# A two-block transformer on one Trainium2 core: where runs of filler matmuls, weight splits and index scores stand in the attention layers

## The chip, the core and the metric

The program runs on one core of one Trainium2 chip. A core has five engines that work side by side, each through its own instruction queue in order: TensorE (PE: matrix products and transposes), VectorE (DVE), ScalarE (ACT), GpSimd (POOL) and SyncE (SP, which here only starts DMA transfers). They wait for one another by semaphores. The metric is the time of one execution on the device in microseconds (us).

## The reference

The input is one sequence of 256 tokens of width 1024, with a memory of 256 rows, all in fp32. Two blocks follow one another. The first has two layers, and each is half a feed-forward part, a mixer and half a feed-forward part; the second has an attention mixer and an expert part. Cut to what matters here:

```python
for i in range(2):                                   # first block
    mem_k, mem_v = split(mem_n @ mem_w_kv[i])
    x = x + 0.5 * swiglu(rmsnorm(x, g0), w_up, w_down)
    h = rmsnorm(x, g1)
    mix = pool_layer(...) if i == 0 else diff_layer(...)
    x = x + mix
    x = x + 0.5 * swiglu(rmsnorm(x, g2), w_up, w_down)

def diff_layer(h, ...):                              # 8 heads, two softmaxes each
    o = (softmax(q1 k1) - lam * softmax(q2 k2)) @ v
    o = rmsnorm(o, norm_g) * (1 - lam_init)
    xo = memory_attention(xq, mem_k, mem_v)          # 4 heads over the memory
    return concat([o, xo]) @ w_out

def hybrid_mixer(h, ...):                            # second block
    # 8 heads over all earlier tokens, 8 heads over the tokens of an index
    score = sum_h iw[h] * relu(iq[h] @ ik)           # 4 index heads
    keep  = top_k(where(causal, score, -inf), 64)    # per query row
    y = concat([moba_attention(...), dsa_attention(..., keep)])
    return y @ w_out
```

## The kernel before, in words

All activations stay on the chip. A matrix product in fp32 is done as three matmuls (`mm3`, L207 to L209) on a high and a low part of both factors. The weights come in chunks of 128 x 1024 values by DMA (`load_to`, L127) as `raw`; ScalarE rounds each to `whi` (`split_one`, L157), VectorE subtracts to get `wlo` (`low_one`, L137; `low_all` does all that are due). The program is one order written out by the Python code: each engine works through its instructions in the order in which the code issues them, so moving a call moves its instructions on every engine that it uses.

In the attention layers a cursor `fill` walks through products that have time (the projections of the next group of heads, then the output product `out_proj_k`), in runs; one `step(fill)` issues one run, and most runs split one chunk ahead (`ahead_one`: `low_all`, then one `split_one`). `pipeline(units, ...)` (L44) walks through the attention units (a unit is a token tile of 128 rows `t` and a pair or group of heads), each cut in steps: s0 scores, bias, row maximum and exponentials; s1 the division by the row sums; s2 the transposes of the probabilities and the copy `pt`; s3 the product with the values; in the diff layer s4 to s6 norm the heads' outputs and transpose them into `cat`. In each tick it takes one step of several units, with two gaps in a tick, and the list `counts` (L993 in the diff layer, L1244 in the second block) says how many runs of `fill` go in each gap.

`out_proj_k` (L420) ends the layers. It adds its product to the rows `x`, half a row (512 columns) at a time, and prepares the following norm: `nxt.pre` scales the half row, `nxt.T` transposes it into `hT_hi` and `hT_lo`, which are what the next block multiplies. A plain norm (`nxt.deep` is false) follows the pool layer and the diff layer.

In the second block `select(t)` computes the index scores of token tile `t` (scores, then eight pairs of MAX and MATCH_REPLACE on VectorE in four steps, then the mask M). Its steps are taken among the runs of the first `aq` and `ak` projections (L1235) and then in the first ticks of the units.

Of the kernel before, what the change touches and what calls it, by code (L numbers as in the profile page):

```python
# [45 lines left out]
def pipeline(units, order):  # L46


    for tick in range(len(units) + max(d for _, d in order)):
        for s, d in order:  # L50
            if s is None:
                yield
                continue
            n = tick - d
            if 0 <= n < len(units) and s < len(units[n]):
                units[n][s]()
        yield
# [3 lines left out]
def kernel(ctx: ExitStack, tc: tile.TileContext, A, LAY, stop=None):  # L61
# [11 lines left out]
    def pmm():  # L73
        return ps.tile([P, 512], F32, name="mm", tag="mm", bufs=4)

    def ptr():
        return ps.tile([P, 512], F32, name="tr", tag="tr", bufs=2)
# [53 lines left out]
    def low_one():  # L131

        j, r, p_ = st["low"].pop(0)
        c = st["s"][j]
        nk, w = items[j][1:3]
        lo = p_.tile([P, CH], F32R, name="wlo", tag="wlo", bufs=4)
        V.tensor_tensor(lo[:, :nk * w], r[:, :nk * w], c.hi.rearrange("p k w -> p (k w)").bitcast(F32), op=OP.subtract)  # L137
        c.lo = lo[:, :nk * w].rearrange("p (k w) -> p k w", w=w)

    def low_all():  # L140
        while st["low"]:
            low_one()

    def split_one():

        j = st["split"]
        load_to(j + cfg["raw"] - len(st["low"]))
        _, nk, w, call = items[j][:4]
        n = nk * w
        r = st["raw"].pop(j)  # L150
        if call is not None:
            call(r[:, :n].rearrange("p (k w) -> p k w", w=w))
        else:
            p_ = wpool2 if j < dense and st["nsplit"] % 2 else wpool
            st["nsplit"] += 1
            hi = p_.tile([P, CH], F32R, name="whi", tag="whi", bufs=4)
            ACT.activation(hi[:, :n], r[:, :n], AF.Copy)  # L157
            st["s"][j] = Split(hi[:, :n].rearrange("p (k w) -> p k w", w=w), None)
            st["low"].append((j, r, p_))
        st["split"] += 1  # L160
        while st["low"] and not cfg["spread"]:
            low_one()
        load_to(j + 1 + cfg["raw"] - len(st["low"]))
# [16 lines left out]
    def ahead_one():  # L180

        if cfg["spread"] and st["split"] < min(st["use"] + 5, len(items)):
            low_all()
            split_one()

    def split_more(n):
        for _ in range(n):
            split_one()

    def fetch(n):  # L190
        got, k = [], 0
        for _ in range(n):
            c, nk, w = nextw()
            got += [(c, kk, k + kk) for kk in range(nk)]
            k += nk
        return got
# [3 lines left out]
    def run_deferred():  # L200
        while deferred:
            deferred.pop(0)()
        for f in strip_hook:
            f()

    def mm3(out, a, b, start, stop):
        PE.matmul(out, a[0], b[0], start=start, stop=False)  # L207
        PE.matmul(out, a[0], b[1], start=False, stop=False)  # L208
        PE.matmul(out, a[1], b[0], start=False, stop=stop)  # L209
# [37 lines left out]
    def proj_cols(act, n, n_ct, evac):  # L247
        got = fetch(n)
        for c0 in range(0, n_ct, 2):
            p = pmm()  # L250
            m = min(2, n_ct - c0)
            for j in range(m):
                if j:
                    ahead_one()
                    yield
                low_all()
                proj_col(act, got, c0 + j, p[:, j * S:(j + 1) * S])
            evac(c0, m, p[:, :m * S].rearrange("p (j t) -> p j t", t=S))
            ahead_one()
            yield  # L260
        run_deferred()
# [6 lines left out]
    def tr(out, in_):  # L268
        PE.transpose(out, in_, ident)
# [150 lines left out]
    def out_proj_k(segs, update, nxt, tail=2, ahead=None):  # L420


        p = [[pmm() for _ in range(2)] for _ in range(NT)]
        n = len(segs)

        def mm(t, h, gis, gots):
            for gi in gis:
                act, k0 = segs[gi]
                for c, k, _ in gots[gi][h]:
                    mm3(p[t][h], act[:, k0 + k, t * P:(t + 1) * P], c[:, k, :], gi == 0 and k == 0, gi == n - 1 and k == 1)  # L430

        gots = {}
        for gi in range(n - tail):
            gots[gi] = [fetch(1), fetch(1)]
            for t in range(NT):
                low_all()
                for h in range(2):
                    mm(t, h, [gi], gots)
                if t:
                    run_deferred()  # L440
                ahead_one()
                yield
        was = dict(cfg)
        cfg.update(ahead=8 - 2 * tail)
        for gi in range(n - tail, n):
            gots[gi] = [fetch(1), fetch(1)]
        cfg.update(was)
        while cfg["spread"] and nxt.deep and st["split"] < st["use"] + 4:
            split_one()
            low_all()  # L450
        for t in range(NT):
            for h in range(2):
                cut = n - 1 if nxt.deep and t and h else n
                mm(t, h, range(n - tail, cut), gots)
                if cut < n:
                    was = dict(cfg)
                    cfg.update(ahead=0)
                    ahead.append(fetch(4))
                    nxt.realT(0)
                    mm(t, h, range(cut, n), gots)  # L460
                    if tail > 2:
                        split_more(1)
                update(t, h, p[t][h])
                nxt.pre(t, h)
                if not nxt.deep and (t or h):
                    nxt.T(*((0, 0), (0, 1), (1, 0))[2 * t + h - 1])
                if h:
                    nxt.stats(t)
                if cut < n:
                    ahead.append(fetch(4))  # L470
                    cfg.update(was)
                if not nxt.deep:
                    ahead_one()
                yield
        if not nxt.deep:
            nxt.late = [lambda: nxt.T(1, 1)]
# [48 lines left out]
    def ffn(n, nxt, stk):  # L525
# [45 lines left out]
        if nxt.deep:  # L571
            flush()
            drain(out_proj_k([(gT, 2 * i) for i in range(11)], half_add, nxt, 3, nxt.got))
        else:
            out_proj(gT, 22, [4, 4, 3], half_add, nxt, first=flush)
# [53 lines left out]
    def step(*gens):  # L629
        for g in gens:  # L630
            next(g, None)
# [155 lines left out]
    with pool("pl") as sp:  # L787
# [53 lines left out]
        counts = [0, 1, 1, 0, 1, 1, 1, 2] + [1] * 6  # L841
# [21 lines left out]
    with pool("df") as sp:  # L863
# [120 lines left out]
        def qk(dst):  # L984
# [5 lines left out]
        o = out_proj_k([(cat, i) for i in range(0, 12, 2)], plain_add, n5)  # L990
        fill = itertools.chain(qk(k[1]), qk(q[1]), v_part(1),
                               proj_cols(hT, 4, 4, lambda c0, m, p: ACT.activation(qx[:, c0:c0 + m, :], p, AF.Copy)), o)
        counts = [1] * 9 + [2, 0, 1, 0, 0, 2, 1, 1, 1, 0, 0] + [1, 0] * 2 + [1, 1, 0, 1, 0, 2]  # L993
        for i, _ in enumerate(pipeline(units, [(5, 6), (1, 2), (4, 4), (None, 0), (6, 6), (0, 0), (3, 3), (2, 2)])):
            for _ in range(counts[i] if i < len(counts) else 1):
                step(fill)
# [147 lines left out]
    def col_evac(dst, b):  # L1144
        return lambda c0, m, p: ACT.activation(dst[:, 4 * b + c0:4 * b + c0 + m, :], p, AF.Copy)
# [81 lines left out]
    se = [select(0), select(1)]  # L1227
    for i, _ in enumerate(itertools.chain(proj_cols(hT, 4, 4, col_evac(aq, 0)), proj_cols(hT, 4, 4, col_evac(ak, 0)))):
        if i == 0:
            for t in range(NT):  # L1230
                q_ = ptr()
                tr(q_[:, :P], iks[t].rearrange("p a b -> p (a b)"))
                ACT.activation(ikT[:, t * P:(t + 1) * P], q_[:, :P], AF.Copy)
        else:
            step(*(se if i == 1 else se[1:] if i == 7 else se[:1]))  # L1235
    nhh = iter(("aq", "ak"))
    m2 = ModNorm(1, None, lambda t: sp.tile([P, D], F32, name="hh2", tag=next(nhh), bufs=1))
    o = out_proj_k([(yA, 0), (yA, 2), (yB, 0), (yB, 2)], Gated(g1), m2, 2, m2.got)
    fill = itertools.chain(proj_cols(hT, 4, 4, col_evac(aq, 1)), proj_cols(hT, 4, 4, col_evac(ak, 1)), v_part(), o)
    units = [make(t, g) for h in range(2) for t in range(NT) for g in (2 * h, 2 * h + 1)]  # L1240
    counts = [1, 0] + [1] * 7 + [0, 2, 0, 1, 0, 2, 0, 1, 0, 2, 1, 0, 0]
    for i, (n, _) in enumerate(zip(counts, pipeline(units, [(1, 2), (None, 0), (3, 3), (2, 2), (0, 0)]))):
        for _ in range(n):
            step(fill)  # L1244
# [306 lines left out]
    for i, (kind, arg) in enumerate(quanta):  # L1551
# [11 lines left out]
        n, t = arg[:2]  # L1563
# [105 lines left out]
def build(nc, arrays, lay, stop=None):  # L1669
    aps = {n: nc.dram_tensor(f"in_{n}_dram", a.shape, mybir.dt.from_np(a.dtype), kind="ExternalInput").ap()  # L1670
           for n, a in arrays.items()}
    aps["out"] = nc.dram_tensor("out_0_dram", (1, S, D), F32, kind="ExternalOutput").ap()
    with tile.TileContext(nc) as tc:
        kernel(tc, aps, lay, stop)
# [11 lines left out]
```

## Time and profile before

| | |
|---|---|
| Time, median of 3 runs | 2088.95 us (2086.64 to 2096.9) |
| The profiled execution | 2091.45 us, of which the span of the trace is 2089.3 us |
| TensorE busy | 2029.2 us, 97% of the span |
| VectorE busy | 1451.0 us, 69% |
| ScalarE busy | 991.4 us, 47% |
| TensorE's granted clock, mean | 0.993 of full speed |

The share of busy time is an average. What a stage costs is read from the gaps of the engine that is busy most, here TensorE: in a timeline of one engine each row has its start, its duration, and in brackets how long the engine was idle before it and what it waited for. The stages that the change touches are the end of the pool layer (about 325 to 360 us of the span), the diff layer's units and end (730 to 912 us) and the second block's attention (1120 to 1245 us).

### The profile page before, as it was taken

How to read it: one execution, taken by the hardware profiler on the slowest of the kernel's cores; microseconds unless marked ns; L12 is line 12 of the kernel's file. 1: busy time of each engine (PE TensorE's matmuls, PEld its weight loads, DVE VectorE, ACT ScalarE, POOL GpSimd, SP SyncE). 2: the span in 40 equal slices, each digit the busy share in tenths (PEclk: the TensorE clock that was granted, in tenths of full speed). 3: DMA queues.
4: the chain of work that ended last, by engine and by line, in shares of the span. 5: the costliest groups of instructions: out<-in, count | busy, mean ns of one | idle time of the engine just before them, and what ended most of it. 6: DMA issues, size and time to landing. Idle time of an engine off the chain costs nothing. (4 is left out here: it accounts for less than half of the span.)

```text
span 2089.3 us, 34420 instructions
## 1 busy us (share of the span) xinstructions
PE 2029.2 (97%) x13678; PEld 1824.7 (87%) x13678; DVE 1451.0 (69%) x2280; ACT 991.4 (47%) x1524; POOL 42.4 (2%) x74
## 2 busy tenths in 40 slices
PE   8999999999999998999999989999999999999998
PEld 7999888998899797789978768999998888888886
DVE  6677566776587557765646888889975666666666
ACT  6444454444344445444444554455554444444444
POOL 2000000000000000000001000000000000000000
PEclk9999999999999999999999999999999999999999
DMA  7667545666577653365544343656776776776764
GB/s 275 213 242 254 189 138 191 240 236 237 190 247 242 212 164 101 117 221 186 204 135 164 112 152 101 192 181 223 244 249 206 220 227 206 230 248 217 223 214 138
DMA packets 142377, 416.92 MB, mean 200 GB/s; under 512 B 12468, under 2 KB 47428, under 8 KB 140040
## 3 DMA queue, kind: packets, MB, share of 16 engines
q1 hardware_dynamic: 102672, 372.04, 53.2%
q10 hardware_dynamic: 37976, 36.91, 5.5%
q0 software_dynamic: 1568, 5.77, 0.9%
q8 instruction: 107, 1.75, 0.3%
q14 instruction: 54, 0.44, 0.1%
HBM read 396.82 MB, written 17.86 MB: 198 GB/s over the span
## 5 line engine op out<-in xcount | busy, mean ns | idle before, releaser
L137 DVE TENSOR_TENSOR wlo<-raw,whi 128x1024 fp32r<-128x1024 f32 (+1 forms) x654 | 784.1, 1221 | 331.3 <-ACT whi L157 330.5
L157 ACT ACTIVATE whi<-raw 128x1024 fp32r<-128x1024 f32 (+1 forms) x654 | 666.1, 1048 | 131.1 <-PE mm L209 66.5
L209 PE MATMUL mm<-hT_hi,wlo 128*128 128x256 f32 x1680 | 472.7, 281 | 8.6 <-DVE wlo L137 8.6
L207 PE MATMUL mm<-hT_hi,whi 128*128 128x256 f32 x1680 | 478.3, 285 | 0.0
L208 PE MATMUL mm<-hT_lo,whi 128*128 128x256 f32 x1680 | 471.7, 281 | 0.0
L209 PEld LDWEIGHTS mm<-hT_hi,wlo 128*128 128x128 f32 x1680 | 317.2, 189 | 10.1 <-DVE wlo L137 10.1
L207 PEld LDWEIGHTS mm<-hT_hi,whi 128*128 128x128 f32 x1680 | 317.3, 189 | 6.1 <-issue 5.5
L208 PEld LDWEIGHTS mm<-hT_lo,whi 128*128 128x128 f32 x1680 | 317.4, 189 | 2.0 <-issue 1.9
L207 PE MATMUL sm<-hT_hi,whi 128*128 128x256 f32 (+1 forms) x1048 | 299.7, 286 | 5.0 <-DVE hT_hi L215 2.5
L209 PE MATMUL sm<-hT_hi,wlo 128*128 128x256 f32 (+1 forms) x1048 | 297.1, 283 | 4.3 <-DVE wlo L137 4.3
L208 PE MATMUL sm<-hT_lo,whi 128*128 128x256 f32 (+1 forms) x1048 | 296.9, 283 | 0.4 <-DVE hT_lo L218 0.4
L207 PEld LDWEIGHTS sm<-hT_hi,whi 128*128 128x128 f32 (+1 forms) x1048 | 199.5, 190 | 8.3 <-DVE hT_hi L215 2.9
L207 PE MATMUL mm<-whi,wh 128*128 128x512 f32 x512 | 202.6, 396 | 2.0 <-ACT wh L217 2.0
L209 PEld LDWEIGHTS sm<-hT_hi,wlo 128*128 128x128 f32 (+1 forms) x1048 | 199.9, 191 | 4.7 <-DVE wlo L137 4.7
L209 PE MATMUL mm<-whi,wl 128*128 128x512 f32 x512 | 202.2, 395 | 0.0
L208 PE MATMUL mm<-wlo,wh 128*128 128x512 f32 x512 | 202.2, 395 | 0.0
L208 PEld LDWEIGHTS sm<-hT_lo,whi 128*128 128x128 f32 (+1 forms) x1048 | 199.3, 190 | 2.9 <-DVE hT_lo L218 0.6
L217 ACT ACTIVATE wh<-wf 128x256 fp32r<-128x256 f32 x128 | 53.5, 418 | 214.9 <-DVE wf L1535 214.9
L207 PE MATMUL mm<-whi,gT_hi 128*128 128x512 f32 x352 | 139.9, 397 | 0.0
L209 PE MATMUL mm<-whi,gT_lo 128*128 128x512 f32 x352 | 139.1, 395 | 0.0
L208 PE MATMUL mm<-wlo,gT_hi 128*128 128x512 f32 x352 | 139.0, 395 | 0.0
L1367 ACT ACTIVATE act<-sm 128x256 f32<-128x256 f32 x128 | 49.2, 385 | 167.9 <-PE sm L209 167.9
(308 smaller groups left out, 2605.4 us busy)
## 6 DMA issues: line engine op xcount, KB each, us to landing
raw<-in_ffn_up_dram SPq DMA_DIRECT2D x176, 512.0 KB, 5.2
raw<-in_peer_u_dram SPq DMA_DIRECT2D x128, 512.0 KB, 4.1
raw<-in_peer_v_dram SPq DMA_DIRECT2D x128, 512.0 KB, 3.7
raw<-in_ffn_dn_dram SPq DMA_DIRECT2D x88, 512.0 KB, 5.1
raw<-in_w_ada_dram SPq DMA_DIRECT2D x48, 512.0 KB, 4.8
gall<-stage ACTq DMA_DIRECT2D x16, 1024.0 KB, 4.8
G<-gall ACTq DMA_DIRECT2D x16, 1024.0 KB, 7.4
raw<-in_diff_w_in_dram SPq DMA_DIRECT2D x28, 512.0 KB, 4.3
```

The lines of the kernel that those rows point to most:

```text
L137: V.tensor_tensor(lo[:, :nk * w], r[:, :nk * w], c.hi.rearrange("p k w -> p (k w)").bitcast(F32), op=OP.subtract)
L157: ACT.activation(hi[:, :n], r[:, :n], AF.Copy)
L207: PE.matmul(out, a[0], b[0], start=start, stop=False)
L208: PE.matmul(out, a[0], b[1], start=False, stop=False)
L209: PE.matmul(out, a[1], b[0], start=False, stop=stop)
L217: ACT.activation(hi, src, AF.Copy)
L1367: ACT.activation(act[n], p, AF.Gelu)
```

## The change

Three edits of order; no operation is added or left out, and the queues of SP and POOL hold the same instructions in the same order as before.

- `out_proj_k`: what is due of `wlo` is done before each product of the tail. With a plain norm, the split of a next chunk (`ahead_one`) stands right behind the product instead of after the norm's work, and for the last half row `wlo` of that chunk follows at once. Between the norm's sums and the last `hT_lo` VectorE's queue then holds four `wlo` at the end of the diff layer, where it held six, and three at the end of the pool layer, where it held five; the others stand ahead of the updates of `x`.
- `counts` of the diff layer: from the tenth gap on, where a gap had two runs and others had none, these are spread, one run a gap.
- The second block: the index scores of tile 1 start one run later (with run 2 instead of run 1, so that tile 0 goes first), and the last of tile 1's pairs move into the ticks of the units; `counts` there has one run in places that had two, and one in places that had none.

```diff
--- before.py
+++ after.py
@@ -451,7 +451,12 @@
         for t in range(NT):
             for h in range(2):
                 cut = n - 1 if nxt.deep and t and h else n
+                low_all()
                 mm(t, h, range(n - tail, cut), gots)
+                if not nxt.deep:
+                    ahead_one()
+                    if t and h:
+                        low_all()
                 if cut < n:
                     was = dict(cfg)
                     cfg.update(ahead=0)
@@ -469,8 +474,6 @@
                 if cut < n:
                     ahead.append(fetch(4))
                     cfg.update(was)
-                if not nxt.deep:
-                    ahead_one()
                 yield
         if not nxt.deep:
             nxt.late = [lambda: nxt.T(1, 1)]
@@ -990,7 +993,7 @@
         o = out_proj_k([(cat, i) for i in range(0, 12, 2)], plain_add, n5)
         fill = itertools.chain(qk(k[1]), qk(q[1]), v_part(1),
                                proj_cols(hT, 4, 4, lambda c0, m, p: ACT.activation(qx[:, c0:c0 + m, :], p, AF.Copy)), o)
-        counts = [1] * 9 + [2, 0, 1, 0, 0, 2, 1, 1, 1, 0, 0] + [1, 0] * 2 + [1, 1, 0, 1, 0, 2]
+        counts = [1] * 9 + [1, 1, 1, 0, 1, 0, 1, 1, 1, 1, 0] + [1, 0] * 2 + [1, 1, 0, 1, 0, 2]
         for i, _ in enumerate(pipeline(units, [(5, 6), (1, 2), (4, 4), (None, 0), (6, 6), (0, 0), (3, 3), (2, 2)])):
             for _ in range(counts[i] if i < len(counts) else 1):
                 step(fill)
@@ -1232,13 +1235,13 @@
                 tr(q_[:, :P], iks[t].rearrange("p a b -> p (a b)"))
                 ACT.activation(ikT[:, t * P:(t + 1) * P], q_[:, :P], AF.Copy)
         else:
-            step(*(se if i == 1 else se[1:] if i == 7 else se[:1]))
+            step(se[i == 2])
     nhh = iter(("aq", "ak"))
     m2 = ModNorm(1, None, lambda t: sp.tile([P, D], F32, name="hh2", tag=next(nhh), bufs=1))
     o = out_proj_k([(yA, 0), (yA, 2), (yB, 0), (yB, 2)], Gated(g1), m2, 2, m2.got)
     fill = itertools.chain(proj_cols(hT, 4, 4, col_evac(aq, 1)), proj_cols(hT, 4, 4, col_evac(ak, 1)), v_part(), o)
     units = [make(t, g) for h in range(2) for t in range(NT) for g in (2 * h, 2 * h + 1)]
-    counts = [1, 0] + [1] * 7 + [0, 2, 0, 1, 0, 2, 0, 1, 0, 2, 1, 0, 0]
+    counts = [1, 0] + [1] * 7 + [0, 1, 1, 1, 0, 1, 1, 1, 0, 1, 1, 1, 0]
     for i, (n, _) in enumerate(zip(counts, pipeline(units, [(1, 2), (None, 0), (3, 3), (2, 2), (0, 0)]))):
         for _ in range(n):
             step(fill)
```

Three places of VectorE's queue (DVE) show what moves. A row reads line, operation, output<-inputs, shape and how many in a row; after the change lines behind L476 stand three higher, so L925 is L928 there. `pt` is the copy of the transposed probabilities (s2), `rc` and `e<-e,rc` are step s1, `ms` and `ov` belong to the norm of the heads (s4, s5), `cat_hi` to s6, and `e<-nd,sm` is the next unit's score.

The first place is in VectorE's queue of the diff layer, in the tick where token tile 0 begins its last two units; before:

```order
L925 COPY pt<-tr 128x512
L137 TENSOR_TENSOR wlo<-raw,whi 128x1024 x2
L907 RECIPROCAL rc<-sum 128x2
L908 RECIPROCAL rc<-sum 128x2
L909 TENSOR_SCALAR rc<-rc,nlam 128x2
L911 TENSOR_SCALAR e<-e,rc 128x256 x2
L913 SCALAR_TENSOR_TENSOR e<-e,rc 128x256 x2
L275 TENSOR_SCALAR ms<-oss 128x4
L891 SCALAR_TENSOR_TENSOR e<-nd,sm 128x128 x4
```

The same place of VectorE's queue now:

```order
L928 COPY pt<-tr 128x512
L137 TENSOR_TENSOR wlo<-raw,whi 128x1024
L910 RECIPROCAL rc<-sum 128x2
L911 RECIPROCAL rc<-sum 128x2
L912 TENSOR_SCALAR rc<-rc,nlam 128x2
L914 TENSOR_SCALAR e<-e,rc 128x256 x2
L916 SCALAR_TENSOR_TENSOR e<-e,rc 128x256 x2
L275 TENSOR_SCALAR ms<-oss 128x4
L137 TENSOR_TENSOR wlo<-raw,whi 128x1024
L894 SCALAR_TENSOR_TENSOR e<-nd,sm 128x128 x4
```

The second `wlo` has moved from ahead of step s1 to behind it.

The second place is some twenty rows further on in the same queue; before:

```order
L925 COPY pt<-tr 128x256
L952 TENSOR_TENSOR ov<-ov,ro 128x512
L907 RECIPROCAL rc<-sum 128x2
L908 RECIPROCAL rc<-sum 128x2
L909 TENSOR_SCALAR rc<-rc,nlam 128x2
L911 TENSOR_SCALAR e<-e,rc 128x128 x2
L913 SCALAR_TENSOR_TENSOR e<-e,rc 128x128 x2
L275 TENSOR_SCALAR ms<-oss 128x4
L137 TENSOR_TENSOR wlo<-raw,whi 128x1024 x2
L221 TENSOR_SCALAR cat_hi<-tr,sng 128x4x128
```

The same place of VectorE's queue now:

```order
L928 COPY pt<-tr 128x256
L137 TENSOR_TENSOR wlo<-raw,whi 128x1024
L955 TENSOR_TENSOR ov<-ov,ro 128x512
L910 RECIPROCAL rc<-sum 128x2
L911 RECIPROCAL rc<-sum 128x2
L912 TENSOR_SCALAR rc<-rc,nlam 128x2
L914 TENSOR_SCALAR e<-e,rc 128x128 x2
L916 SCALAR_TENSOR_TENSOR e<-e,rc 128x128 x2
L275 TENSOR_SCALAR ms<-oss 128x4
L221 TENSOR_SCALAR cat_hi<-tr,sng 128x4x128
```

One `wlo` has moved up, directly behind the copy `pt`, and none stands ahead of `cat_hi` any more.

The third place is in VectorE's queue in the attention of the second block, at the units' first ticks; `score` and `m` are tile 1's index scores and the eight values found, M the mask. Before:

```order
L1137 MAX m_11580<-score 128x8
L1138 MATCH_REPLACE score<-m_11580,score 128x256
L1137 MAX m_11583<-score 128x8
L1138 MATCH_REPLACE score<-m_11583,score 128x256
L1194 RECIPROCAL rc_11586<-sum_11481 128x4
L1198 TENSOR_SCALAR e<-e,rc_11586 128x128 x2
L137 TENSOR_TENSOR wlo<-raw,whi 128x1024
L1141 TENSOR_SCALAR M<-score 128x256
L1210 COPY pt<-tr 128x512
L1181 SCALAR_TENSOR_TENSOR e<-sm,strip 128x512 x2
L1188 TENSOR_REDUCE mx_11637<-e 128x2 x2
L137 TENSOR_TENSOR wlo<-raw,whi 128x1024
```

The same place of VectorE's queue now:

```order
L1201 TENSOR_SCALAR e<-e,rc_11580 128x128 x2
L137 TENSOR_TENSOR wlo<-raw,whi 128x1024
L1140 MAX m_11617<-score 128x8
L1141 MATCH_REPLACE score<-m_11617,score 128x256
L1140 MAX m_11620<-score 128x8
L1141 MATCH_REPLACE score<-m_11620,score 128x256
L1213 COPY pt<-tr 128x512
L1184 SCALAR_TENSOR_TENSOR e<-sm,strip 128x512 x2
L1191 TENSOR_REDUCE mx_11636<-e 128x2 x2
L137 TENSOR_TENSOR wlo<-raw,whi 128x1024
L1144 TENSOR_SCALAR M<-score 128x256
```

The pair of MAX and MATCH_REPLACE twice over now stands between that unit's division and its copy `pt`, and the mask M, which stood there, comes after the next unit's reduction and a `wlo`.

## Rows read from the trace of the kernel before

**Rows 1.** The page's first part: busy us, share of the span, instructions by engine.

```profile
PE 2029.2 (97%) x13678; PEld 1824.7 (87%) x13678; DVE 1451.0 (69%) x2280; ACT 991.4 (47%) x1524; POOL 42.4 (2%) x74
```

**Rows 2.** Windows: busy us and instructions of each engine, granted clock, DMA share, GB/s.

```profile
730.00:912.00 182.00, 169.65 (x1083) 148.60 (x1083) 129.73 (x263) 89.07 (x198) 11.11 (x11) 0.97 0.43 141
1182.00:1224.00 42.00, 39.66 (x236) 29.77 (x233) 35.00 (x65) 23.73 (x56) 0.00 (x0) 1.00 0.34 107
```

**Rows 3.** Timeline of PE, diff layer: start, duration, instruction, idle before, releaser.

```profile
810.02 1.09 PE L269 MATMUL tr<-ident,e 128*128 128x128 f32 x4 [2.19 <-DVE e L913]
...
823.54 0.58 PE L209 MATMUL mm<-hT_hi,wlo 128*128 128x256 f32 x1 [3.91 <-DVE wlo L137]
...
844.70 0.63 PE L269 MATMUL tr<-ident,e 128*128 128x128 f32 x4 [0.98 <-DVE xscale L594]
...
893.62 0.49 PE L208 MATMUL mm<-wlo,hT_hi 128*128 128x512 f32 x1 [2.02 <-DVE wlo L137]
```

**Rows 4.** Windows behind three of these restarts, columns as in rows 2.

```profile
809.74:813.15 3.41, 3.13 (x10) 2.63 (x11) 3.34 (x13) 1.45 (x7) 1.04 (x1) 0.50 0.38 138
823.39:826.80 3.41, 3.25 (x15) 3.26 (x16) 1.24 (x2) 0.00 (x0) 0.97 (x1) 0.50 0.61 192
895.07:898.48 3.41, 3.41 (x11) 2.73 (x11) 3.33 (x4) 1.33 (x3) 0.00 (x0) 0.50 0.86 262
```

**Rows 5.** Timeline of DVE, diff layer.

```profile
807.20 1.23 DVE L137 TENSOR_TENSOR wlo<-raw,whi 128x1024 fp32r<-128x1024 f32 x1 [2.92 <-ACT whi L157]
...
809.39 0.88 DVE L913 SCALAR_TENSOR_TENSOR e<-e,rc 128x256 f32<-128x256 f32 x2
...
818.89 0.42 DVE L925 COPY pt<-tr 128x256 f32<-128x256 f32 x1
...
822.27 2.35 DVE L137 TENSOR_TENSOR wlo<-raw,whi 128x1024 fp32r<-128x1024 f32 x2
...
892.35 7.06 DVE L137 TENSOR_TENSOR wlo<-raw,whi 128x1024 fp32r<-128x1024 f32 x6
899.33 0.68 DVE L218 TENSOR_TENSOR hT_lo<-tr,hT_hi 128x512 fp32r<-128x512 f32 x1
```

**Rows 6.** Timeline of ACT, end of the diff layer.

```profile
897.09 1.06 ACT L157 ACTIVATE whi<-raw 128x1024 fp32r<-128x1024 f32 x1 [1.85 <-DMA raw<-in_ffn_up_dram]
```

**Rows 7.** Timeline of PE, end of the pool layer.

```profile
349.97 0.50 PE L208 MATMUL mm<-wlo,hT_hi 128*128 128x512 f32 x1 [0.63 <-DVE wlo L137]
```

**Rows 8.** Timeline of DVE, end of the pool layer.

```profile
348.70 5.76 DVE L137 TENSOR_TENSOR wlo<-raw,whi 128x1024 fp32r<-128x1024 f32 x5
```

**Rows 9.** Timeline of PE, attention of the second block.

```profile
1127.20 1.40 PE L1123 MATMUL sm<-ikT,iqT 64*128 64x256 f32 x8 [1.25 <-ACT rel L1125]
...
1167.87 0.38 PE L209 MATMUL mm<-hT_hi,wlo 128*128 128x256 f32 x1 [1.21 <-DVE wlo L137]
...
1206.89 1.10 PE L1175 MATMUL sm<-ak,aq 64*128 64x256 f32 x4 [1.42 <-DVE hT_lo L218]
...
1208.26 0.40 PE L208 MATMUL mm<-wlo,yA_hi 128*128 128x512 f32 x1
...
1210.54 0.39 PE L209 MATMUL mm<-whi,yA_lo 128*128 128x512 f32 x1
...
1213.08 0.84 PE L269 MATMUL tr<-ident,e 128*128 128x128 f32 x4 [0.74 <-ACT e L1200]
...
1234.11 1.06 PE L269 MATMUL tr<-ident,hh 128*128 128x128 f32 x8 [1.05 <-DVE hh L363]
```

**Rows 10.** Timeline of DVE, attention of the second block.

```profile
1159.83 0.42 DVE L1137 MAX8 m<-score 128x8 f32<-128x256 f32 x1
...
1161.35 0.41 DVE L1138 MATCH_REPLACE8 score<-m,score 128x256 f32<-128x256 f32 x1
...
1163.41 0.29 DVE L1141 TENSOR_SCALAR M<-score 128x256 f32<-128x256 f32 x1
...
1222.53 5.75 DVE L137 TENSOR_TENSOR wlo<-raw,whi 128x1024 fp32r<-128x1024 f32 x5
```

## The prediction, on record before the changed kernel ran

> **What bounds the kernel now.** I read the busy times first: TensorE is busy 2029.2 us of 2089.3, VectorE 1451.0 [rows 1]. So the sum is TensorE's, and an order can only save TensorE's gaps and what lies at a lower clock behind them. Next I read the windows of the touched stages: in the diff layer TensorE is busy 169.65 of 182 us, at a mean clock of 0.97 [rows 2]; 12 us of gaps are there. Then TensorE's timeline with the releaser of each gap. In the diff layer four gaps stand out: 2.19 us for `e` of step s1, 3.91 us for a `wlo`, 0.98 us for `xscale`, 2.02 us for a `wlo` at the layer's end [rows 3]. VectorE released all four, and its own timeline says why: a `wlo` that itself waited 2.92 us for `whi` stands ahead of s1, and the `wlo` of 822.27 stands behind the unit's whole tail [rows 5]. After the three longer gaps a stretch has a granted clock of 0.50, which is 1.2 instead of 2.4 GHz [rows 4]. A restart after a long gap costs the gap and half of what TensorE was busy in the slow stretch: 3.13 / 2 = 1.6 us, 3.25 / 2 = 1.6, 3.41 / 2 = 1.7. The attention has gaps of 1.25, 1.21, 1.42, 0.74 and 1.05 us [rows 9], none of them with a slow stretch: from 1182 to 1224 us the clock is 1.00 [rows 2]. The pool layer's end has one, 0.63 us [rows 7].
>
> **The change part by part.** The sum is made against the profiled execution, 2091.45 us (span 2089.3); it lies 2.5 us above the median of the runs shown, 2088.95, and the differences are carried over to that median. Nothing is added on any engine, so only gaps and clock count.
>
> *Diff layer, `counts`.* First place: VectorE finished `wlo` at 808.43 and then s1, whose last row ends at 809.39 + 0.88 = 810.27, so s1 takes 1.84 us after it [rows 5]; the transposes start at 810.02 on its first results [rows 3]. With s1 ahead of that `wlo`, s1 runs in the 2.92 us in which VectorE was idle. The gap of 2.19 and its slow stretch of 1.6 go, and TensorE comes 3.8 us earlier to what follows. Second place: the product waits for the first of two `wlo`, whose end is 822.27 + 1.2 = 823.5 [rows 5]. Now it goes directly behind `pt`, which ended at 818.89 + 0.42 = 819.31: there it would end at 820.5, and VectorE itself is earlier by the 2.4 us or so that the first place gives it less what the moved `wlo` takes, so I expect 818.1. The product restarts there instead of at 823.54: 5.4 us earlier. That includes the first place's 3.8: what is left of them is bound by VectorE and comes back as new gaps, about 0.5 us for a transpose and 1.8 us for the `wlo`. The slow stretch behind the 3.91 gap is gone as well, 1.6. Then the transposes behind it wait about 1.3 us for `cat_lo`, which is still behind s1. Together -5.4 - 1.6 + 1.3 = -5.7. The gap of 0.98 becomes 0.8, since one more `wlo` stands ahead of `cat_hi`: -0.2. Diff units: -5.9. Bounds: all three gaps and two slow stretches gone and nothing back, -10.3; from the other side, each of the three new gaps brings a slow stretch of 1.6, -1.1.
>
> *Norm ends, `out_proj_k`.* In the diff layer's end six `wlo` take 7.06 us and the last `hT_lo` stands behind them at 899.33 [rows 5]. With two of them earlier, the gap of 2.02 and the slow stretch of 1.7 behind it go: -3.7. But the last of the remaining four needs a `whi` that ScalarE starts at 897.09, when its raw chunk has landed [rows 6], so `hT_lo` stays near 899.3 whatever the order, and TensorE, now early, waits for it. I give back 1.5: -2.2. Bounds: -3.7 if that chunk lands earlier, because ScalarE frees `raw` buffers one piece earlier; 0 if all comes back. What hides the moved `wlo` ahead of the updates of `x`: a run of 12 matmuls of 128x512 takes 12 x 0.23 = 2.8 us (ten intervals from 1208.26 to 1210.54 [rows 9]) while `wlo` and the update take about 2; if that cover fails, 1.2 us, one `wlo`, for each. At the pool's end the five `wlo` of 348.70 [rows 8] become three; the gap of 0.63 goes, and a little of what follows: -0.8, between -1.5 and +0.6 by the same reckoning.
>
> *Second block, index scores.* The scores of tile 1 no longer follow those of tile 0 at once, so the gap of 1.25 for `rel` [rows 9] goes; VectorE's work behind it comes hardly earlier, and the next `wlo` gives half back: -0.7 (0 to -1.25). The last two pairs of tile 1 move to a place where VectorE is the one waited for: from 1159.83 to 1161.35 + 0.41 = 1161.76 they took 1.93 us, and the mask that stood there took 0.29 [rows 10], so the `wlo` behind comes 1.93 - 0.29 = 1.64 us later. TensorE already waited 1.21 for it [rows 9]: all 1.64 are on the path. The gap grows to about 3 us, which lies among those that brought a slow stretch (2.02 to 3.91 [rows 3]) and above those that brought none (to 1.42 [rows 9]): +1.6. Bounds 0 and +3.3.
>
> *Second block, `counts`.* One run a gap gives the early unit steps shorter cover and the later ones some that they lacked: the gaps of 1.42 and 0.74 [rows 9] go, -2.2, and +0.9 comes back at gaps that had two runs. In this stretch VectorE is busy 35.00 of 42 us [rows 2], so it has 7 us to spare, and it is not in deficit on the whole. -1.3 (-2.2 to +2.8, a whole run of 12 uncovered). At the end, five `wlo` of 5.75 us stood ahead of the updates of `x` [rows 10] and led to the wait of 1.05 for `hh` [rows 9]; they now stand partly earlier: -0.9 (-1.5 to -0.3). The attention: -0.7 + 1.64 + 1.6 - 1.3 - 0.9 = +0.3.
>
> **Sum:** -5.9 - 2.2 - 0.8 + 0.3 = -8.6 us. From the median, 2088.95 - 8.6 = 2080.4 us (a profiled execution like the one shown would be at 2082.9).
>
> **A rule against the change.** What the rows say: the single runs from 1182 to 1224 us kept the clock at 1.00, and only gaps from 2.02 us on had a stretch at 0.50 [rows 2 to 4]. The Trainium skill, "Perfetto Trace Analysis", section "Matmul Optimizations", says that the matmul engine scales its power with utilisation and that matmuls should therefore run back to back in batches. By that rule, cutting runs of two into single ones is a step in the wrong direction; by the rows it is not, as long as the gaps stay short. The traces bear it out only for long gaps, and it is rival 2.
>
> **The rivals.**
> 1. *Waits that go do not come back.* The VectorE chain turns out loose in the diff layer. Then 2.19 + 3.91 + 0.98 + 2.02 = 9.1 and slow stretches of 1.6 + 1.6 + 1.7 = 4.9 go, and the pool's 0.6: -14.6; the attention +0.3. 2088.95 - 14.3 = 2074.7. For it: VectorE is busy only 129.73 of 182 us there [rows 2]. Against it: at exactly these places its rows stand back to back.
> 2. *Short batches bring slow stretches.* Five new short gaps of the forecast (0.5, 1.8 and 1.3 in the diff units, 1.5 at its end, 0.9 in the attention) have one each at about 1.5: +7.5. 2080.4 + 7.5 = 2087.9. For it: the diff layer has three such stretches. Against it: gaps of 0.98 to 1.42 had none; only two of the five are above that.
> 3. *Slower: the attention's cover.* If unit scores that had 24 matmuls of cover have 12 and VectorE does not keep up, three ticks lose 2.8 each, with a slow stretch of 1.5 each: +12.9 in place of -1.3. 2080.4 + 14.2 = 2094.6. It decides from about 2 such ticks, where 8.6 are used up. Against it: the 7 us that VectorE has to spare there [rows 2]; for it: that the two pairs push VectorE back just ahead of them.
>
> **How the numbers follow.** The forecast has 0.60, its own range -4.5 to -12.5, so 2076.5 to 2084.5. Rival 1 has 0.16, rival 2 0.16, rival 3 0.08. Half a per cent is 10.4 us, about what a measurement of this kernel can tell from no change: faster means under 2078.5, slower over 2099.4. Faster: all but a little of rival 1, 0.14, and nearly a third of the forecast, 0.18, so 0.32. Slower: the upper part of rival 3, 0.04. Same: 0.64. For 8 in 10, the range takes in rival 1 below and rival 2 above and leaves out rival 3 and what lies beyond rival 1: 2073 to 2089.5.
>
> **What would show it.** In the changed kernel's timeline of TensorE: no gap for `e` before the transposes near 808 us, and no stretch at clock 0.50 there; the product that waited until 823.54 restarting near 818 by then behind a gap under 2 us; a wait for `hT_lo`, not for `wlo`, at the end of the diff layer; no wait for `rel`; and in the attention, near 1168 us less what was gained before, a gap of about 3 us for `wlo` with a slow stretch. The forecast is wrong if these gaps keep their length in another place (rival 2 or 3), or if the diff layer and its end together gain much more than 8 or much less than 4 us.

## The result, and the profile after

| | before | changed |
|---|---|---|
| Time, median | 2093.18 us (2086.64 to 2096.9, 6 runs) | 2080.72 us (2077.01 to 2082.93, 6 runs) |
| Ratio | | 0.9944, 95% interval 0.9931 to 0.9956 |
| Profiled execution, span | 2091.45, 2089.3 us | 2077.22, 2075.4 us |
| TensorE's granted clock, mean | 0.993 | 0.995 |

The forecast was 2080.4 us, and the measured time is 2080.72. That agreement is luck: with more runs the kernel before stands at 2093.18 instead of 2088.95, so the change is worth 0.0056 x 2093 = 11.7 us (9.2 to 14.4), where 8.6 was forecast. The direction and the range held; the size was somewhat too small.

The page's first part of the changed kernel, as in [rows 1], shows TensorE 6.5 us less busy for the same 13678 matmuls. Part of that is that fewer of them run at the lower clock (granted mean 0.995 for 0.993):

```profile
PE 2022.7 (97%) x13678; PEld 1819.8 (88%) x13678; DVE 1451.7 (70%) x2280; ACT 990.9 (48%) x1524; POOL 41.7 (2%) x74
```

The windows of the pool layer's end, of the diff layer and of the attention (columns as in [rows 2]). The diff layer took 182 us at a mean clock of 0.97 and now takes 171.9 at 1.00; the pool's end has no gap left:

```profile
325.00:360.60 35.60, 35.60 (x178) 29.27 (x177) 20.55 (x28) 17.67 (x27) 3.56 (x3) 1.00 0.46 152
728.90:900.80 171.90, 165.31 (x1083) 145.00 (x1083) 129.62 (x263) 88.67 (x198) 10.30 (x11) 1.00 0.46 151
1109.00:1232.00 123.00, 114.34 (x792) 96.19 (x791) 100.74 (x197) 65.32 (x144) 4.99 (x4) 1.00 0.41 135
```

TensorE's timeline of the changed kernel at the places of [rows 3]. The gap of 2.19 us for `e` and that of 0.98 for `xscale` have no row any more; 3.91 became 1.66, and 2.02 for `wlo` became 0.99 for `hT_lo`; and there is a new one, 0.62 for `cat_lo`:

```profile
816.76 0.38 PE L209 MATMUL mm<-hT_hi,wlo 128*128 128x256 f32 x1 [1.66 <-DVE wlo L137]
820.41 0.41 PE L269 MATMUL tr<-ident,e 128*128 128x128 f32 x2 [0.62 <-DVE cat_lo L224]
...
890.22 0.50 PE L209 MATMUL mm<-whi,hT_lo 128*128 128x512 f32 x1 [0.99 <-DVE hT_lo L218]
```

VectorE's timeline there, as in [rows 5]. Step s1 now ends before the `wlo` that waits for `whi`, the `wlo` that TensorE waits for next starts at 815.49, right behind `pt`, and four `wlo` instead of six stand ahead of the last `hT_lo`:

```profile
804.15 0.87 DVE L916 SCALAR_TENSOR_TENSOR e<-e,rc 128x256 f32<-128x256 f32 x2
...
806.09 1.23 DVE L137 TENSOR_TENSOR wlo<-raw,whi 128x1024 fp32r<-128x1024 f32 x1 [0.99 <-ACT whi L157]
...
815.49 1.22 DVE L137 TENSOR_TENSOR wlo<-raw,whi 128x1024 fp32r<-128x1024 f32 x1
...
884.93 4.63 DVE L137 TENSOR_TENSOR wlo<-raw,whi 128x1024 fp32r<-128x1024 f32 x4
889.48 0.68 DVE L218 TENSOR_TENSOR hT_lo<-tr,hT_hi 128x512 fp32r<-128x512 f32 x1
```

TensorE's waits in the attention (us in total, times, the longest). Before, two rows of them were

```profile
PE mm L209 <- DVE wlo L137: 2.6, 3, 1.2
PE tr L269 <- DVE e L1198: 1.6, 1, 1.6
```

In the changed kernel those for `rel` and for `hT_lo` in [rows 9] are gone and the one for `hh` is short, the one of 1.6 us for `e` stays, and `wlo` takes 5.0 us instead of 2.6:

```profile
PE mm L209 <- DVE wlo L137: 5.0, 3, 2.9
PE tr L269 <- DVE e L1201: 1.6, 1, 1.6
PE tr L269 <- ACT e L1203: 0.9, 1, 0.9
PE mm L207 <- DVE hT_hi L215: 0.8, 1, 0.8
PE tr L269 <- DVE hh L363: 0.4, 2, 0.2
```

Both kernels issue the same number of matmuls. So the time of a stage can be compared between two traces: count TensorE's matmuls, and take the starts of the same two of them, one at each end of the stage. By that, against the trace before, in us (the second trace of the changed kernel is from a later run, below):

| stage | forecast | changed | changed, second trace |
|---|---|---|---|
| pool layer's end | -0.8 | -1.06 | -1.04 |
| diff units | -5.9 | -7.53 | -7.49 |
| diff layer's end | -2.2 | -2.60 | -2.61 |
| attention | +0.3 | -2.18 | +0.92 |
| all the rest | 0 | -0.6 | +1.8 |
| whole | -8.6 | -13.97 | -8.40 |

### The profile page after: what moved, and what is told of

Its sections match the earlier page's. It is cut to its first block, busy times and chain, and to the rows that moved or that the text cites. A ratio compares the mean times of both kernels' runs of the same rounds, so it can differ in the third digit from the quotient of the medians.

```text
span 2075.4 us, 34428 instructions
## 1 busy us (share of the span) xinstructions
PE 2022.7 (97%) x13678; PEld 1819.8 (88%) x13678; DVE 1451.7 (70%) x2280; ACT 990.9 (48%) x1524; POOL 41.7 (2%) x74
```

## The experiments

**One part at a time.** Four kernels, each the kernel before with one part of the change, timed on one chip. The edits are the hunks of the change: those of `out_proj_k` (norm_only); and

```diff
# diff_counts_only
-        counts = [1] * 9 + [2, 0, 1, 0, 0, 2, 1, 1, 1, 0, 0] + ...
+        counts = [1] * 9 + [1, 1, 1, 0, 1, 0, 1, 1, 1, 1, 0] + ...
# index_only
-            step(*(se if i == 1 else se[1:] if i == 7 else se[:1]))
+            step(se[i == 2])
# attention_counts_only
-    counts = [1, 0] + [1] * 7 + [0, 2, 0, 1, 0, 2, 0, 1, 0, 2, 1, 0, 0]
+    counts = [1, 0] + [1] * 7 + [0, 1, 1, 1, 0, 1, 1, 1, 0, 1, 1, 1, 0]
```

> The kernel before with the edits of out_proj_k alone. Theory (each edit shortens the gaps of its own stage, and the stages add up): the pool layer's end gains 1.0 to 1.4 us, the diff layer's end 2.0 to 2.6 us, the diff units and the attention within 0.2 us of before; in all -3.0 to -4.0 us, ratio 0.998 to 0.9987. Rival (the split's earlier place helps because the pieces run earlier through all that follows): the diff units would also come 1 us or more earlier relative to their start. Rival (what moves in time is where gaps meet the clock): stages that the edit does not touch differ by 0.9 to 1.7 us either way, and the total by as much from the sum of its stages.

> The kernel before with the new counts of the diff layer alone. Theory: the gap of 2.19 us for e goes, the gap of 3.91 us for wlo becomes about 1.7, the gap of 0.98 us for xscale goes, and no stretch at half clock follows any of them; the diff units gain 7.0 to 8.0 us. The diff layer's end keeps its gap of about 2.0 us. In all -7 to -8 us, ratio 0.9962 to 0.9967. Rival (part of the changed kernel's gain in the diff units came from the edits of out_proj_k, whose low_all also stands in the layer's last runs): 5 us or less here.

> The kernel before with the index scores of tile 1 one run later, alone. Theory (the pairs' 1.64 us that VectorE does later lie on the path): the gap of 1.25 us for rel goes, half of it comes back at the next wlo, and the gap before the wlo that was 1.21 us becomes 2.8 to 3.0 us; the attention is 1.0 to 1.3 us longer than before, 1.6 us more if a stretch at half clock follows the long gap. Rival (the move is worth something: the scores' gap is saved and the pairs are hidden): the attention 0.4 to 1.2 us shorter.

> The kernel before with the new counts of the second block's attention alone. Theory: the gaps of 1.42 us for hT_lo and of 1.05 us for hh go, the one of 0.74 us stays about as it is, no stretch at half clock comes; the attention gains 3.0 to 3.6 us, ratio 0.9983 to 0.9987. Rival (the change of the counts is worth something only with the index scores moved): 1.5 us or less. Rival (shorter cover costs): slower by 2 us or more.

| run | median | ratio to before, 95% | own stage, by trace |
|---|---|---|---|
| norm_only | 2089.81 us | 0.9987 (0.9978 to 0.9996) | pool's end -1.06, diff layer's end -2.61 |
| diff_counts_only | 2083.93 us | 0.9963 (0.9949 to 0.9976) | diff units -6.85 |
| index_only | 2093.93 us | 1.0006 (0.9995 to 1.0017) | attention +0.81 |
| attention_counts_only | 2088.80 us | 0.9983 (0.9974 to 0.9993) | attention -3.32 |

The parts add up: the product of the four ratios is 0.9939, the changed kernel has 0.9944. The rivals that let one part depend on another fall. norm_only and attention_counts_only came as expected by stage, diff_counts_only a little under its 7.0 to 8.0 us, index_only a little under its 1.0 to 1.3.

In norm_only the diff units keep both their gaps, and the layer's end shows the 0.99 us of the changed kernel (TensorE's timeline):

```profile
808.62 1.08 PE L269 MATMUL tr<-ident,e 128*128 128x128 f32 x4 [2.25 <-DVE e L916]
...
822.22 0.58 PE L209 MATMUL mm<-hT_hi,wlo 128*128 128x256 f32 x1 [3.91 <-DVE wlo L137]
...
897.56 0.50 PE L209 MATMUL mm<-whi,hT_lo 128*128 128x512 f32 x1 [0.99 <-DVE hT_lo L218]
```

In diff_counts_only it is the other way round, the gaps of the units nearly as in the changed kernel and the end as in the kernel before:

```profile
817.10 0.39 PE L209 MATMUL mm<-hT_hi,wlo 128*128 128x256 f32 x1 [1.66 <-DVE wlo L137]
...
886.00 0.74 PE L208 MATMUL mm<-wlo,hT_hi 128*128 128x512 f32 x1 [2.02 <-DVE wlo L137]
```

One thing expected of it failed: that no slow stretch would follow. Behind the gap of 1.66 us the clock is 0.50, and so it is once in its attention, 2 us behind the restart from the gap of 1.42 us. In the changed kernel neither place has one. The first is the likely reason why the units gain 0.7 us less here than there: of the runs further below with the same counts, index_old_spread alone has a stretch at 0.50 in the units, and they gain 6.8 us there, in all others 7.5:

```profile
817.83:821.24 3.41, 3.41 (x14) 2.27 (x15) 3.05 (x10) 1.82 (x6) 1.01 (x1) 0.50 0.50 154
1200.12:1203.53 3.41, 3.41 (x10) 2.34 (x8) 3.38 (x8) 1.73 (x7) 0.00 (x0) 0.50 0.00 0
```

One warning stands in norm_only: its whole trace is 7.37 us shorter than the trace before, its timing only 0.13%, 2.7 us. 3.7 of the 7.37 lie in stages that the edit does not touch, and the traced execution is the fastest of its eleven. The rival that untouched stages differ too holds there, for single traces, and by more than the 0.9 to 1.7 us that it named.

A second warning concerns the trace before itself. index_only and attention_counts_only leave the diff layer as it was, and at its end they have the gap for `wlo` of before, 2.03 us, but no slow stretch behind it. Windows behind it in these two:

```profile
893.85:897.26 3.41, 3.41 (x17) 2.81 (x18) 3.41 (x4) 1.63 (x2) 1.11 (x3) 1.00 0.68 213
893.17:896.58 3.41, 3.41 (x17) 2.81 (x18) 3.41 (x4) 1.63 (x2) 1.11 (x3) 1.00 0.62 210
```

There the layer's end takes 1.3 us less than in the trace before. So half of the -2.6 us of the layer's end is a shorter wait, and half is a slow stretch that only two of the four traces with the old end have (before and diff_counts_only).

index_only by time can't be told from the kernel before. Its trace shows where the move costs. The gap for `rel` is gone, 0.76 us up to the first units, and 1.57 are lost behind them. But not as expected: the gap before the `wlo` did not grow to 2.9 us. TensorE's timeline has 1.32 there, and ahead of it a stretch at a mean clock of 0.64:

```profile
1161.70 0.79 PE L269 MATMUL tr<-ident,e 128*128 128x128 f32 x4 [1.65 <-DVE e L1198]
...
1168.98 0.38 PE L209 MATMUL mm<-hT_hi,wlo 128*128 128x256 f32 x1 [1.32 <-DVE wlo L137]
```

```profile
1161.70:1166.40 4.70, 4.70 (x23) 3.78 (x24) 4.60 (x11) 1.84 (x4) 0.00 (x0) 0.64 0.43 146
```

VectorE sets when the product goes on; TensorE's slow stretch only filled a wait that would have been there anyway. The changed kernel has the same move, a gap of 2.85 us and no slow stretch ahead of it, and loses 1.62 us at the same place. The two are not to be added. The same trace shows it in part at the first two places of the diff layer, which it does not touch: behind the gap of 2.19 the clock stays at 1.00, and the next gap is 4.50 us instead of 3.91. From the transposes to the product it takes 12.81 us there instead of 13.52, so the slow stretch of the trace before cost 0.7 us and otherwise filled the wait:

```profile
809.76 0.74 PE L269 MATMUL tr<-ident,e 128*128 128x128 f32 x4 [2.19 <-DVE e L913]
...
822.57 0.58 PE L209 MATMUL mm<-hT_hi,wlo 128*128 128x256 f32 x1 [4.50 <-DVE wlo L137]
```

```profile
809.70:813.10 3.40, 3.33 (x16) 2.55 (x16) 3.33 (x12) 1.66 (x9) 1.04 (x1) 1.00 0.34 135
```

attention_counts_only did as its theory said. The waits from 1180 us on are down to these, the one of 1.42 us for `hT_lo` is gone, no slow stretch came, and the rival that shorter cover costs time falls:

```profile
PE tr L269 <- ACT e L1200: 0.9, 1, 0.9
PE mm L207 <- DVE hT_hi L215: 0.8, 1, 0.8
PE tr L269 <- DVE hh L363: 0.2, 1, 0.2
```

**Where the index scores should stand.** If VectorE is short of time only at the units' first ticks, tile 1's pairs belong elsewhere. Five more kernels start from the changed one; after_index_old takes back the line of index_only, the others are

```diff
# index_both_run7
-            step(se[i == 2])
+            step(*(se if i == 7 else [se[i == 2]]))
# index_pairs_spread (index_old_spread: the old line, gaps 2, 4, 6, then 8)
-        if 1 <= i <= 4:
+        if i in (2, 4, 6, 8):
             step(se[1])
-        elif i == 5:
+        elif i == 10:
             drain(*se)
# index_best: index_both_run7, and
-        if 1 <= i <= 4:
+        if i in (1, 2, 6):
             step(se[1])
-        elif i == 5:
+        elif i == 8:
             drain(*se)
```

> The changed kernel with the index scores' runs as they were before (tile 1 starts together with tile 0, three pairs are left for the units); norm ends and both counts stay changed. Theory (of the three edits only the move of the index scores costs: 0.8 us saved at rel, 1.6 lost where VectorE is the bound): the gap for rel of 1.25 us comes back, the gap of 2.85 us before wlo shrinks to 1.2, and the attention (to the product behind it) is 0.8 to 1.3 us shorter than in the changed kernel; ratio to the kernel before 0.9936 to 0.9942. Rival (the new counts of the attention need the moved scores): the attention 1 us or more longer.

> The changed kernel, but run 7 of the first projections steps both index scores, so the first pairs of tile 1 stand before the units, in a stretch in which VectorE waits 1.89 us for whi, and three pairs are left for the units as in the kernel before. Theory (a pair costs TensorE its 1.93 us only where VectorE is saturated): no gap for rel, the gap of 2.85 us becomes 1.2, the attention is 1.4 to 1.9 us shorter than in the changed kernel. Rival (VectorE only carries the backlog on): within 0.5 us of the changed kernel.

> The changed kernel, but tile 1's four steps of pairs stand in every second gap of the units (gaps 2, 4, 6, 8, the mask at 10) instead of in gaps 1 to 4; they are needed by tile 1's units at gap 12. Theory (the pairs cost where VectorE is saturated, at ticks 0 to 2, where it is busy 14.09 of 15 us, and nothing at ticks 3 to 5, where TensorE has no gap): the gaps of 1.61 us for e and of 2.85 us for wlo lose 3 us together, the attention is 2.5 to 3.5 us shorter than in the changed kernel. Rival (VectorE is short of time in the whole attention, so the wait only moves): the gaps come back behind 1160 us and the attention is within 0.7 us of the changed kernel.

> As the run with the index scores' runs of before, but with the three remaining pairs of tile 1 in gaps 2, 4 and 6 and the mask at 8. Theory (as for the spread pairs): the gap for rel of 1.25 us is back, no gap over 1 us for e or wlo from 1145 to 1165 us, the attention 2.3 to 3.5 us shorter than in the changed kernel, so about as good as the spread pairs with the moved scores. Rival (VectorE short throughout): within 1 us of the changed kernel.

> The changed kernel with both index scores stepped at run 7 (one pair fewer left for the units), two of tile 1's three remaining pairs in gaps 1 and 2, the last in gap 6 and the mask in gap 8, so that none stands in gaps 3 to 5, where VectorE is the one waited for. Theory (a pair costs its 1.93 us just where VectorE is saturated and nothing where TensorE is the bound): the gap of 1.61 us for e and that of 2.85 us for wlo both fall below 0.5 us, the gap of 1.59 us for wlo at the first projections stays, and the attention is 3.5 to 4.5 us shorter than in the changed kernel; ratio to the kernel before 0.991 to 0.9925. Rival (VectorE carries a backlog, and a pair left out at one place shows as a wait at the next): 2.2 us or less, as in the two runs that moved the pairs by one place.

| run | median | ratio to before, 95% | attention, by trace |
|---|---|---|---|
| changed | 2080.72 us | 0.9944 (0.9931 to 0.9956) | -2.18 |
| after_index_old | 2078.56 us | 0.9933 (0.9919 to 0.9947) | -3.27 |
| index_both_run7 | 2076.09 us | 0.9924 (0.9911 to 0.9937) | -4.01 |
| index_pairs_spread | 2076.90 us | 0.9925 (0.9911 to 0.9938) | -4.09 |
| index_old_spread | 2077.72 us | 0.9930 (0.9917 to 0.9942) | -4.34 |
| index_best | 2076.93 us | 0.9928 (0.9914 to 0.9941) | -4.61 |

In the changed kernel the last step of tile 1's pairs, MAX and MATCH_REPLACE twice over, stands ahead of the `wlo` with the gap of 2.85 us, back to back (VectorE's timeline; compare [rows 10]):

```profile
1151.94 0.42 DVE L1140 MAX8 m<-score 128x8 f32<-128x256 f32 x1
...
1153.46 0.41 DVE L1141 MATCH_REPLACE8 score<-m,score 128x256 f32<-128x256 f32 x1
...
1156.76 1.22 DVE L137 TENSOR_TENSOR wlo<-raw,whi 128x1024 fp32r<-128x1024 f32 x1
```

Without it (after_index_old, index_both_run7) the gap falls from 2.85 to 1.21 us, 1.64 less, as the 1.93 us of the two pairs less the mask's 0.29 say. after_index_old is 1.09 shorter than the changed kernel, index_both_run7 1.83, both as expected: by trace, the move of the index scores was the one part of the change that cost. (By time after_index_old alone can't be told from the changed kernel, since the intervals overlap.) Spreading the pairs gained 1.9 us and 2.2 where 2.5 to 3.5 and 2.3 to 3.5 were expected, and index_best 2.4 instead of 3.5 to 4.5. In both spread kernels the gap for `e` went, but one of 2.2 us for `wlo` was left, where none over 1 us was expected of index_old_spread. In index_best the rival (2.2 us or less) was nearly right: with no pair at the saturated ticks, the waits of TensorE in index_best are

```profile
PE mm L209 <- DVE wlo L137: 3.3, 3, 1.7
PE tr L269 <- ACT e L1203: 1.7, 2, 0.9
PE mm L207 <- DVE hT_hi L215: 0.8, 1, 0.8
PE tr L269 <- DVE hh L363: 0.2, 1, 0.2
```

The wait for `e` is still 0.86 us, now for ScalarE, and that for `wlo` 1.11: taking VectorE's work away shows the next engine in the chain, not zero. All five beat the kernel before. Which of the five is best can't be told by time, since their intervals cover one another; that the last beats the changed kernel is seen in the next pair of runs.

**The changed kernel again**, beside index_best on the same chip.

> The changed kernel as it is, beside the run before on the same chip, for a direct comparison. Stages that no edit touches differ between traces of the same order: theory (slow stretches fall by where gaps meet the clock): the stages that the change touches come within 0.3 us of its first trace, the rest of the span differs by 0.5 to 3 us. Rival (the differences in the untouched stages come from the change): the rest is within 0.3 us too. Ratio to the kernel before 0.993 to 0.996.

2081.50 us (2079.32 to 2082.79), ratio 0.9946 (0.9933 to 0.996); index_best beside it 2076.93 (2076.05 to 2077.99), 4.6 us less, and no run of the one lies among those of the other. The pool's end and the diff layer repeat within 0.05 us, and the rest differs by 2.4. But my theory missed in the attention, which the change does touch: +0.92 after -2.18. The gaps are the same to 0.1 us (TensorE's timeline, second trace), and behind two of them the windows of the second trace show a clock near 0.5:

```profile
1158.69 0.58 PE L209 MATMUL mm<-hT_hi,wlo 128*128 128x256 f32 x1 [2.85 <-DVE wlo L137]
...
1194.96 0.62 PE L269 MATMUL tr<-ident,e 128*128 128x128 f32 x2 [0.88 <-ACT e L1203]
```

```profile
1158.70:1162.10 3.40, 3.40 (x16) 3.40 (x17) 1.94 (x5) 1.86 (x5) 0.00 (x0) 0.52 0.46 157
1195.90:1199.30 3.40, 3.40 (x12) 2.26 (x11) 2.63 (x5) 0.73 (x1) 0.00 (x0) 0.53 0.45 147
```

In the first trace the same two places, behind the same two gaps, have 1.00:

```profile
1158.00:1161.40 3.40, 3.37 (x28) 3.35 (x28) 1.98 (x5) 1.90 (x5) 0.00 (x0) 1.00 0.48 157
1192.50:1195.90 3.40, 3.11 (x15) 2.25 (x16) 3.00 (x7) 1.95 (x4) 0.00 (x0) 1.00 0.46 154
```

So the order is one thing and the clock behind a gap another: the two slow stretches cost about 1.5 and 1.6 us in this execution (by so much the stages from 1145 to 1185 us and from 1185 to 1245 us of the trace before are longer than in the first trace), and the other execution has none.

## Why the prediction was right, and where it was not

- **The pool layer's end.** Right, -1.06 for -0.8: its one gap is gone and none came instead.
- **First place of the diff units.** Right for the gap: the 2.19 us for `e` are gone, with s1 run in the time in which VectorE had waited for `whi`. The slow stretch behind it was priced at 1.6 and is worth 0.7 (index_only, above); the sum did not suffer, since it bound this place by the next one.
- **Second place.** Right: the product was to restart near 818.1 in the time of the trace before. It restarts at 816.76, plus the 1.12 us that the changed kernel is ahead when the units begin: 817.9. The gap of 1.8 is 1.66; the one of 0.5 for a transpose did not come.
- **What comes back behind it.** Mis-sized: 1.3 us were given back for `cat_lo`, and it is 0.62; 0.8 for the gap at `xscale`, and it is gone. Those two terms, 0.7 + 0.8, are nearly all of the 1.6 us by which the diff units beat the forecast (-7.53 for -5.9). That VectorE had more slack behind the second place than I gave it is how I read this; no run tests it.
- **The diff layer's end.** The size came out (-2.6 for -2.2), the reason not. The -3.7 counted a gap of 2.02 and a slow stretch of 1.7; measured, the wait shrank by 1.0 to one for `hT_lo`, and the slow stretch was worth 1.3, which two of four executions of the old order do not pay at all. As to the wait that is left, I had the last `hT_lo` held at its time by a raw chunk's arrival. In the changed kernel ScalarE makes the last of those `whi` from 886.69 on without a wait, right behind the ones before it, and VectorE does its four `wlo` back to back: the wait is for VectorE's own queue. ScalarE's timeline of the changed kernel, where a wait would stand in brackets:

```profile
883.85 2.94 ACT L157 ACTIVATE whi<-raw 128x1024 fp32r<-128x1024 f32 x3
...
886.69 1.05 ACT L157 ACTIVATE whi<-raw 128x1024 fp32r<-128x1024 f32 x1
```

- **Index scores.** The gap for `rel` gave 0.4 in the changed kernel and 0.76 in index_only, for 0.7. The 1.64 us of the two pairs came exactly (1145 to 1185 us is 1.62 longer). The step that failed is the +1.6 for a slow stretch behind the gap of about 3 us: none came in the first trace, one came in the second, and in index_only one came ahead of the gap and lay inside VectorE's time. It should have stood with a chance, not as a certain term. I also passed over the longest gap of this stage, 1.56 us for `e` without a slow stretch behind it; it stayed, at 1.61. TensorE's timeline before:

```profile
1162.22 0.79 PE L269 MATMUL tr<-ident,e 128*128 128x128 f32 x4 [1.56 <-DVE e L1198]
```

- **The attention's counts.** -2.2 was forecast for counts and tail together; 3.4 came. Of the gaps, 1.42 went, but 0.74 did not: a wait of 0.88 us for ScalarE's `e` stands there, about the 0.9 that was given back. From 1185 to 1216 us TensorE's idle time fell by 1.4, as forecast (-1.3), and the stage by 2.06; the other 0.7 is matmuls that take less time, 0.6 of it the 24 score products of L1175, and no run shows why. The tail gave 1.3 for 0.9.
- **Rivals.** Rival 3 fell with attention_counts_only. Rival 1 is nearer than I gave it: in the diff layer 10.1 us went, of the 14.0 that it counts there. Rival 2 was put wrongly. I argued that gaps of up to 1.42 us have no slow stretch; in the changed kernel's second trace one of 0.88 us does, and in diff_counts_only those of 1.42 and 1.66. The shorter batches of the new order do not by themselves bring one, since the first trace has the same batches and gaps without one. The Trainium skill, "Perfetto Trace Analysis", section "Matmul Optimizations", says that the matmul engine scales its power with utilisation and that matmuls should therefore run back to back in batches. By that, cutting runs of two into single ones should have cost clock, which it did not here: the diff layer's mean rose from 0.97 to 1.00 while its waits became shorter, and of the eight traces with the new counts six have no stretch at 0.50 in the diff units and two have one, while each of the four with the old counts has one or two. What decides whether a given gap is followed by a slow stretch stays open; these runs show only that its length alone does not.
- **What a measurement can tell.** I put that at half a per cent, 10.4 us. The interval of the ratio is 0.25% wide, so this change of 0.56% is clear of noise.

## What to carry to other kernels

Where two engines alternate, put the work that must wait for a third behind the work whose inputs are ready: the new counts of the diff layer, which do this with single `wlo`, were worth more than all the rest (alone a ratio of 0.9963, where the whole change has 0.9944; no run moves one `wlo` alone). Price a slow stretch of the clock with a chance, and at less where another engine sets the next start: here 1.3 to 1.6 us where TensorE set it, and 0 to 0.7 where VectorE did. Judge a change of half a per cent by timed medians and by stages, position for position in one engine's order, not by one trace's whole span; and look in each stage for slow stretches that one of the two traces happens to have.

## What the runs showed that was not expected

- Two executions of one program with the same gaps to 0.1 us differ by 3.1 us in the attention, and the clock is what differs: 1.00 in one trace, 0.52 and 0.53 in the other behind gaps of 2.85 and 0.88 us.
- Outside the four stages of the table, the trace of norm_only was 4.0 us shorter than the trace before, that of after_index_old 3.4 us longer.
- The same wait of 2.0 us at the end of the diff layer, in the same order, was followed by a slow stretch in two traces and by none in two others, and that is worth 1.3 us.
